# A decoder trunk on one core: the norm chains rewritten (products with the weights ahead of the factor, sums of squares by halves, GpSimd only for the power), and weight splits let three steps ahead instead of four

## The chip, the cores and the metric

The kernel runs on one core of a Trainium2 chip. Its time is the device time of one execution in microseconds (us), from the program's start to its end on that core. The engines are TensorE (PE; its weight loads are shown apart as PEld), VectorE (DVE), ScalarE (ACT), GpSimd (POOL) and SyncE (SP), which here issues transfers from HBM.

## The reference, cut to what matters

Two layers; in each an FFN, a mixer and a second FFN. Before each of the six stages the input passes through an RMS norm with weights, behind each the output passes through a second one and is added to x. x is 256 tokens by 1024, in f32.

```python
def rms_norm(x, gain):
    y = x * lax.rsqrt(jnp.mean(x * x, axis=-1, keepdims=True) + NORM_EPS)
    return y * gain
def swiglu(x, wg, wu, wd):
    return (jax.nn.silu(x @ wg) * (x @ wu)) @ wd
for l in range(DEPTH):
    x = x + 0.5 * rms_norm(swiglu(rms_norm(x, g_ffn1_pre[l]), ffn1_wg[l], ffn1_wu[l], ffn1_wd[l]), g_ffn1_post[l])
    x = x + rms_norm(hybrid_mixer(rms_norm(x, g_mix_pre[l]), ...), g_mix_post[l])
    x = x + 0.5 * rms_norm(swiglu(rms_norm(x, g_ffn2_pre[l]), ffn2_wg[l], ...), g_ffn2_post[l])
```

The mixer merges three attentions (differential, stick-breaking, block-sparse) with sigmoid gates; the change touches in it only the norm of the differential one.

## The kernel before, in words

The 256 tokens are two tiles (t = 0, 1) of 128 partitions, and x stays in SBUF as `x_73` (tile 0) and `x_74` (tile 1). The six stages are numbered n = 0 to 5; a name such as `f20Tl` says FFN (f) or mixer (m, with the layer's number), stage 2, tile 0, and the quantity. FFNs are n = 0, 2, 3, 5; the mixers are m0 (n = 1) and m1 (n = 4).

**Weights.** SP loads them in blocks of 128 x 2048 f32 (1 MB, `raw`, five buffers). Each block is split into a high and a low part, by halves of 128 x 1024: ACT copies the high part `whi` (L143), DVE subtracts for the low part `wlo` (L144). A product in f32 accuracy is three matmuls: high by high (L339), high by low (L341), low by high (L344). Activations are split in the same way after their transposition on PE: `f20p` is the transposed tile in PSUM, `f20Th` its high part (ACT, L273), `f20Tl` its low part (DVE, L274), and `f20q` a copy kept for sums (ACT, L276). The FFNs' up products of pairs of chunks are done with seven products in place of eight, for which DVE adds whole weight blocks (L134, `raw<-raw,raw`) and forms four sums of activations.

**Which split comes when.** `Stream` holds the list of uses of the weights; before each use `ahead` (L150 on) emits splits up to `AHEAD` uses ahead of the current one (L41, L154), as far as the five split buffers allow. The first five steps are in hand-written order on ACT and DVE; all else is placed by a scheduler that works by priority, which is the order of the program, except that what stands in a `soon()` block counts as if it stood 200 instructions earlier. A change of the program's order or of a chain's length so also changes which matmuls the scheduler sets between others.

**The norm chains.** `sumsq` lets ACT square a tile and accumulate the sum (two instructions, ACTIVATE and ACTIVATION_READ_ACCUMULATOR, both L229). `rstd_of` forms the factor on POOL: one `tensor_scalar` for each sum (L221: times 1/n, plus eps or plus the sum so far), then a power of -0.5 (L223). `postnorm` sums the output `acc` (PSUM) by halves, waits for the factor, forms y = acc * factor * weights (L323, a scalar_tensor_tensor of 128 x 512 for each half), then x = x + y (L325). `normed` (before an FFN) sums x in one instruction of 128 x 1024, and forms `xg` = x * factor * weights (L296, two halves); PE transposes `xg` (L271). Before a mixer, `gained` forms x * weights without the factor (L288), which is applied later (`m00r`, and `m00rq` on POOL, L711).

**Order at a stage's end.** Tile 0 of a stage ends ahead of tile 1, and tile 1's last matmuls run while tile 0's post and pre norms do; the next stage begins with tile 0's transposes, its first up products (`f20gu`), the first of the seven products (`f2c1X`), then tile 1's transposes (`f21p`). Behind an up product ACT takes the Silu `f20h` (L425) and DVE multiplies (L426).

Of the kernel before, what the change touches and what calls it, by code (L numbers as in the profile page):

```python
# [9 lines left out]
F32 = mybir.dt.float32  # L10
F32R = mybir.dt.float32r
BF16 = mybir.dt.bfloat16
AF = mybir.ActivationFunctionType
ALU = mybir.AluOpType
# [3 lines left out]
P = 128  # L18
D = 1024
# [10 lines left out]
EPS = 1e-6  # L30
# [7 lines left out]
HALF = BLK // 2  # L38
W_BUFS = 5
RAW_BUFS = 5  # L40
AHEAD = 4  # L41
LAG = 3
WARM = 18
SECOND_HALF = 2
# [8 lines left out]
HALVES = (slice(0, D // 2), slice(D // 2, D))  # L53
# [5 lines left out]
class Stream:  # L59
# [90 lines left out]
    def ahead(self, most):  # L150

        while self.done < len(self.ops) and most > 0:
            k = self.ops[self.done][0]
            if self.first[k] > self.now + AHEAD or not self.room(k):  # L154
                return
# [10 lines left out]
def trunk(ctx: ExitStack, tc, x, wall, gpre, gpost, lamv, dgain, cst, out):  # L166
    nc = tc.nc
# [3 lines left out]
    sp = ctx.enter_context(tc.tile_pool(name="act", bufs=2))  # L171
# [3 lines left out]
    def tr_tile(shape, name, tag=None):  # L175
        return ps.tile(shape, F32, tag=tag or next(tr_tags), name=name, bufs=1)
# [5 lines left out]
    xs = [cp.tile([P, D], F32, tag=f"x{t}", name=f"x{t}") for t in range(NT)]  # L182
# [14 lines left out]
    def gain(kind, i):  # L197

        if (kind, i) not in gains:
            src = gpre if kind == "pre" else gpost  # L200
            g = sp.tile([P, D], F32, tag="gain", name=f"g{kind}{i}", bufs=2)
            nc.sync.dma_start(g, bass.AP(tensor=src.tensor, offset=src.offset + i * D,
                                         ap=[[0, P], [1, D]]))
            gains[kind, i] = g
        return gains[kind, i]
# [7 lines left out]
    dg = cp.tile([P, L], F32, tag="dg", name="dg")  # L213
    nhalf = cp.tile([P, 4], F32, tag="nhalf", name="nhalf")
    nc.gpsimd.memset(nhalf, -0.5)
    def rstd_of(ssq, n, k, scale, name, tag="rstd"):

        r = sp.tile([P, k], F32, tag=tag, name=name, bufs=4)
        plus = EPS * scale ** -2
        for s in ssq:  # L220
            nc.gpsimd.tensor_scalar(r, s, scale ** -2 / n, plus, op0=ALU.mult, op1=ALU.add)  # L221
            plus = r
        nc.gpsimd.tensor_tensor(r, r, nhalf[:, :k], op=ALU.pow)  # L223
        return r

    def sumsq(src, n, name):
        junk = sp.tile([P, n], F32, tag="t4", name=name + "j", bufs=4)
        s = sp.tile([P, 1], F32, tag="ssq", name=name + "s", bufs=4)
        nc.scalar.activation(junk, src, AF.Square, accum_out=s)  # L229
        return s  # L230

    side, waiting = [], []
# [8 lines left out]
    def rest(n):  # L241
        for _ in range(n):
            yield
# [11 lines left out]
    def soon():  # L255
        return tc.high_priority(offset=SOON)

    def pair(nk, name, tag, bufs):
        if nk == 2:
            both = sp.tile([P, 2, nk, P], F32R, tag=tag, name=name, bufs=bufs)  # L260
            return [both[:, 0], both[:, 1]]
        if tag == "xT":
            return [sp.tile([P, nk, P], F32R, tag=tag + c, name=name + c, bufs=bufs) for c in "hl"]
        return [sp.tile([P, nk, P], F32R, tag=tag, name=name + c, bufs=bufs) for c in "hl"]

    def split_T(src, dst, a, n, name, keep=None):

        hi, lo = (d[:, a:a + n] for d in dst[:2])
        pt = tr_tile([P, 4, P], name, "tr" if name[0] == "f" and n == 2 else None)
        for k in range(n):  # L270
            nc.tensor.transpose(pt[:, k, :], src[:, (a + k) * P:(a + k + 1) * P], ident)  # L271
        with soon():
            nc.scalar.activation(hi, pt[:, :n], AF.Copy)  # L273
            nc.vector.tensor_sub(lo, pt[:, :n], hi.bitcast(F32))  # L274
            if keep is not None:
                nc.scalar.activation(keep[:, a:a + n], pt[:, :n], AF.Copy)  # L276
# [5 lines left out]
    xg, quads = {}, {}  # L282

    def gained(t, i, c):

        if t not in xg:
            xg[t] = sp.tile([P, D], F32, tag="t4", name=f"xg{i}{t}", bufs=4)
        nc.vector.tensor_mul(xg[t][:, c], xs[t][:, c], gain("pre", i)[:, c])  # L288

    def normed(t, i):  # L290

        with soon():
            r = rstd_of([sumsq(xs[t], D, f"n{i}{t}")], D, 1, 1.0, f"n{i}{t}r", "rpre")
            xg[t] = sp.tile([P, D], F32, tag="t4", name=f"xg{i}{t}", bufs=4)
            for c in HALVES:
                nc.vector.scalar_tensor_tensor(xg[t][:, c], xs[t][:, c], r, gain("pre", i)[:, c],  # L296
                                               op0=ALU.mult, op1=ALU.mult)

    def prenorm(t, i, name, keep=False):

        src = xg.pop(t)
        if keep:
            r, quads[t] = None, sp.tile([P, KD, P], F32, tag="t4", name=name + "q", bufs=4)
        else:
            r = rstd_of([sumsq(xs[t], D, name)], D, 1, 1.0, name + "r", "rpre")
        xT = pair(KD, name + "T", "xT", NT)
        yield xT, r
        for a in (0, 4):
            split_T(src, xT, a, 4, f"{name}p{a}", quads[t] if keep else None)
            yield  # L310

    def postnorm(t, acc, i, scale, name):

        y = sp.tile([P, D], F32, tag="t4", name=name + "y", bufs=4)
        with soon():
            r = rstd_of([sumsq(acc[:, c], D // 2, name + str(n)) for n, c in enumerate(HALVES)],
                        D, 1, scale, name + "r")
        g = gain("post", i)
        for c in HALVES:
            if c.start:  # L320
                yield
            with soon():
                nc.vector.scalar_tensor_tensor(y[:, c], acc[:, c], r, g[:, c],  # L323
                                               op0=ALU.mult, op1=ALU.mult)
                nc.vector.tensor_add(xs[t][:, c], xs[t][:, c], y[:, c])  # L325
                if i + 1 == 3 * L:
                    nc.scalar.dma_start(out[t * P:(t + 1) * P, c], xs[t][:, c])
                elif (i + 1) % 3 == 1:
                    gained(t, i + 1, c)
        if i + 1 < 3 * L and (i + 1) % 3 != 1:  # L330
            normed(t, i + 1)
        yield
# [218 lines left out]
    def groups(t):  # L551

        per = 8 // (t + 1)
        return [range(g * per, (g + 1) * per) for g in range(t + 1)]
# [36 lines left out]
    def diff_attention(y, t, l, qT, name):  # L591
        yield
        po = sp.tile([P, 4, P], F32, tag="tok", name=name + "o", bufs=4)
        for g, ms in enumerate(groups(t)):
            e, r = softmax(t, "a", qT, ms, f"{name}g{g}")
            yield from rest(REST_DIFF)
            n = len(ms) // 2
            lr = sp.tile([P, n], F32, tag="lr", name=f"{name}lr{g}")
            nc.vector.tensor_scalar(lr, r[:, 1, :], lam[:, l:l + 1], None, op0=ALU.mult)
            for i in range(n):  # L600
                nc.vector.tensor_scalar(e[:, 1, i, :], e[:, 1, i, :], lr[:, i:i + 1], None,
                                        op0=ALU.mult)
                nc.vector.scalar_tensor_tensor(e[:, 0, i, :], e[:, 0, i, :], r[:, 0, i:i + 1],
                                               e[:, 1, i, :], op0=ALU.mult, op1=ALU.subtract)
            yield
            wT = maps_T(e, range(0, 2 * n, 2), t, f"{name}T{g}")
            yield from rest(REST_MAPS)
            pa = tr_tile([P, n, P], f"{name}a{g}")
            for i in range(n):
                h = ms[0] // 2 + i  # L610
                for kb in range(t + 1):
                    nc.tensor.matmul(pa[:, i, :], wT[2 * i, kb], vS["a", kb][:, h * P:(h + 1) * P],
                                     start=kb == 0, stop=kb == t, skip_group_check=True)
            nc.scalar.activation(po[:, ms[0] // 2:ms[0] // 2 + n, :], pa, AF.Copy)
            yield
        sq = sp.tile([P, 4, P], F32, tag="tok", name=name + "sq", bufs=4)
        nc.scalar.activation(sq, po, AF.Square)
        ssq = sp.tile([P, 4], F32, tag="ssq4", name=name + "ssq")
        nc.vector.tensor_reduce(ssq, sq, axis=AX.X, op=ALU.add)
        rs = rstd_of([ssq], P, 4, 1.0, name + "rs")  # L620
        nc.vector.tensor_mul(po, po, rs[:, :, None].to_broadcast([P, 4, P]))
        yield from rest(REST_NORM)
        pt = tr_tile([P, 4, P], name + "at")
        for h in range(4):
            nc.tensor.transpose(pt[:, h, :], po[:, h, :], ident)
        nc.scalar.activation(y[0], pt, AF.Copy, scale=dg[:, l:l + 1])
        nc.vector.scalar_tensor_tensor(y[1], pt, dg[:, l:l + 1], y[0].bitcast(F32), op0=ALU.mult,
                                       op1=ALU.subtract)
# [351 lines left out]
```

## Time and profile before

| | us |
|---|---|
| three runs | 1275.62, 1277.13, 1277.08 |
| median | 1277.08 |
| profiled execution | 1277.28 |
| its span (first to last instruction) | 1275.3 |

The granted TensorE clock is 0.995 of full speed over the whole execution. In the profile's groups the largest are DVE's `wlo` (496 instructions, 588.9 us), ACT's `whi` (496, 503.2 us) and DVE's block sums (96, 115.6 us). How to read it: a group's row names line, engine, operation and operands, then busy time and the idle time of that engine just ahead of it; a row of the timeline has start and duration in us, and in brackets how long its engine had been idle and what the instruction waited for. Rows of one kind that follow on each other are drawn together (x2), with one duration over all.

### The profile page before, as it was taken

How to read it: one execution, taken by the hardware profiler on the slowest of the kernel's cores; microseconds unless marked ns; L12 is line 12 of the kernel's file. 1: busy time of each engine (PE TensorE's matmuls, PEld its weight loads, DVE VectorE, ACT ScalarE, POOL GpSimd, SP SyncE). 2: the span in 40 equal slices, each digit the busy share in tenths (PEclk: the TensorE clock that was granted, in tenths of full speed). 3: DMA queues.
4: the chain of work that ended last, by engine and by line, in shares of the span. 5: the costliest groups of instructions: out<-in, count | busy, mean ns of one | idle time of the engine just before them, and what ended most of it. 6: DMA issues, size and time to landing. Idle time of an engine off the chain costs nothing.

```text
span 1275.3 us, 15584 instructions
## 1 busy us (share of the span) xinstructions
PE 1249.8 (98%) x6034; PEld 1014.9 (80%) x6034; DVE 984.5 (77%) x1233; ACT 789.1 (62%) x1149; POOL 52.2 (4%) x82
## 2 busy tenths in 40 slices
PE   7999999999999999999999999999999999999997
PEld 4888887888877878888878888878888787788885
DVE  5999967656566589999599998666665656999982
ACT  6566655678676476666466655556885655666551
POOL 0000003000000010000010000210000000100000
PEclk8999999999999999999999999999999999999999
DMA  9465465443444434476435458454344544264550
GB/s 345 169 250 202 174 250 210 153 160 138 171 159 166 159 138 174 158 262 251 179 132 205 191 198 321 160 180 165 132 155 153 183 154 166 98 226 174 195 198 33
DMA packets 34057, 232.37 MB, mean 182 GB/s; under 512 B 3904, under 2 KB 4032, under 8 KB 6976
## 3 DMA queue, kind: packets, MB, share of 16 engines
q1 hardware_dynamic: 33264, 230.28, 49.8%
q10 hardware_dynamic: 720, 1.11, 0.2%
q8 instruction: 47, 0.77, 0.2%
q14 instruction: 26, 0.21, 0.0%
HBM read 230.33 MB, written 1.05 MB: 181 GB/s over the span
## 4 chain that ended last, share of the span: by engine, by line
PE 90%; DVE 4%; POOL 3%; issue 1%; ACT 1%; DMA 1%; SPq 0%; POOLq 0%; DVEq 0%; ACTq 0%
DVE wlo L144 1%; PE f01gu L344 1%; PE f00acc L339 1%; PE f51gu L339 1%; PE f51gu L344 1%; PE f30acc L339 1%; PE f31gu L339 1%; PE f50acc L339 1%; PE f31gu L344 1%; PE f51acc L339 1%; PE f00acc L341 1%; PE f30acc L341 1%; PE f20acc L341 1%; PE f20acc L344 1%; PE f00acc L344 1%
## 5 line engine op out<-in xcount | busy, mean ns | idle before, releaser
L144 DVE TENSOR_TENSOR wlo<-raw,whi 128x1024 fp32r<-128x1024 f32 x496 | 588.9, 1219 | 101.7 <-ACT whi L143 101.1
L143 ACT ACTIVATE whi<-raw 128x1024 fp32r<-128x1024 f32 x496 | 503.2, 1055 | 170.8 <-DVE raw L134 23.0
L134 DVE TENSOR_TENSOR raw<-raw,raw 128x1024 f32<-128x1024 f32 x96 | 115.6, 1217 | 0.0
L339 PE MATMUL f00gu<-whi,f00Th 128*128 128x512 f32 x40 | 17.2, 430 | 2.1 <-ACT f00Th L273 1.9
L721 ACT ACT_TABLE_LOAD x12 | 15.4, 1283 | 6.2 <-PE m11bg L344 2.2
L344 PE MATMUL f50gu<-whi,f50Tl 128*128 128x512 f32 x40 | 15.8, 394 | 1.2 <-DVE f50Tl L274 1.2
L344 PE MATMUL f20gu<-whi,f20Tl 128*128 128x512 f32 x40 | 15.8, 394 | 1.2 <-DVE f20Tl L274 1.2
L341 PE MATMUL f00gu<-wlo,f00Th 128*128 128x512 f32 x40 | 16.5, 412 | 0.4 <-DVE wlo L144 0.4
L344 PE MATMUL f00gu<-whi,f00Tl 128*128 128x512 f32 x40 | 16.5, 414 | 0.2 <-DVE f00Tl L274 0.2
L344 PE MATMUL f01gu<-whi,f01Tl 128*128 128x512 f32 x40 | 15.8, 394 | 0.7 <-DVE f01Tl L274 0.7
L339 PE MATMUL f00acc<-whi,f00hT 128*128 128x512 f32 x40 | 16.2, 404 | 0.0
L575 ACT ACT_TABLE_LOAD x6 | 7.7, 1283 | 13.6 <-DVE m01cg1m L570 3.6
L339 PE MATMUL f20gu<-whi,f20Th 128*128 128x512 f32 x40 | 16.1, 403 | 0.0
L339 PE MATMUL f30gu<-whi,f30Th 128*128 128x512 f32 x40 | 16.1, 403 | 0.0
L339 PE MATMUL f50gu<-whi,f50Th 128*128 128x512 f32 x40 | 16.1, 402 | 0.0
L339 PE MATMUL f30acc<-whi,f30hT 128*128 128x512 f32 x40 | 16.1, 402 | 0.0
L339 PE MATMUL f21gu<-whi,f21Th 128*128 128x512 f32 x40 | 16.0, 401 | 0.0
L339 PE MATMUL f51gu<-whi,f51Th 128*128 128x512 f32 x40 | 16.0, 400 | 0.0
L339 PE MATMUL f20acc<-whi,f20hT 128*128 128x512 f32 x40 | 16.0, 400 | 0.0
L339 PE MATMUL f31gu<-whi,f31Th 128*128 128x512 f32 x40 | 16.0, 400 | 0.0
L339 PE MATMUL f01gu<-whi,f01Th 128*128 128x512 f32 x40 | 16.0, 400 | 0.0
L339 PE MATMUL f50acc<-whi,f50hT 128*128 128x512 f32 x40 | 16.0, 399 | 0.0
(1990 smaller groups left out, 3556.6 us busy)
## 6 DMA issues: line engine op xcount, KB each, us to landing
raw<-wall_dram SPq DMA_DIRECT2D x211, 1024.0 KB, 4.8
gpre<-gpre_dram SPq DMA_DIRECT2D x6, 512.0 KB, 5.2
gpost<-gpost_dram SPq DMA_DIRECT2D x6, 512.0 KB, 4.0
raw<-wall_dram SPq DMA_DIRECT2D x2, 512.0 KB, 7.8
out_dram<-x ACTq DMA_DIRECT2D x4, 256.0 KB, 2.1
x<-x_dram SPq DMA_DIRECT2D x2, 256.0 KB, 2.9
x<-x_dram SPq DMA_DIRECT2D x1, 512.0 KB, 9.0
cs<-cst_dram SPq DMA_DIRECT2D x1, 352.0 KB, 6.3
```

The costliest lines, as they stand in the source:

```text
L134: nc.vector.tensor_add(self.raws[op[1]][:, c], self.raws[op[1]][:, c], self.raws[op[2]][:, c])
L143: nc.scalar.activation(hi, w, AF.Copy)
L144: nc.vector.tensor_sub(lo, w, hi.bitcast(F32))
L339: nc.tensor.matmul(o[:, n:n + 512], xh[:, k, :], wh[:, kk, n:n + 512], start=first, stop=False, **kw)
L341: nc.tensor.matmul(o[:, n:n + 512], xh[:, k, :], wl[:, kk, n:n + 512], start=False, stop=False, **kw)
L344: nc.tensor.matmul(o[:, n:n + 512], xl[:, k, :], wh[:, kk, n:n + 512], start=False, stop=last, **kw)
L575: nc.scalar.activation(e[:, b, i, :], s[:, b, i, :], AF.Exp, bias=mn[:, b, i:i + 1], scale=-1.0, accum_out=sm[:, b, i:i + 1])
L721: nc.scalar.activation(s, o, AF.Sigmoid, scale=r)
```

## The change

- `AHEAD` is 3 instead of 4.
- `rstd_of`: DVE's `tensor_scalar` (L219 of the changed kernel) adds eps and, where there are two sums, both sums in one instruction; POOL takes only the power. The mean's 1/n goes into the scale of ACT's Square.
- `normed`: the squares are taken by halves (two instructions of 128 x 512), and their unused output goes into `xg`'s own tile, ahead of `xg` itself.
- `postnorm`: y = acc * weights is formed ahead of the factor (L322, reads PSUM), and then one instruction makes x = y * factor + x (L327), instead of L323 and L325.

```diff
-AHEAD = 4
+AHEAD = 3
-    def rstd_of(ssq, n, k, scale, name, tag="rstd"):
+    def rstd_of(ssq, k, name, tag="rstd", eps=EPS):
         r = sp.tile([P, k], F32, tag=tag, name=name, bufs=4)
-        plus = EPS * scale ** -2
-        for s in ssq:
-            nc.gpsimd.tensor_scalar(r, s, scale ** -2 / n, plus, op0=ALU.mult, op1=ALU.add)
-            plus = r
+        nc.vector.tensor_scalar(r, ssq[0], eps, *ssq[1:] or [None], op0=ALU.add,
+                                **({"op1": ALU.add} if ssq[1:] else {}))
         nc.gpsimd.tensor_tensor(r, r, nhalf[:, :k], op=ALU.pow)
...
     def normed(t, i):
         with soon():
-            r = rstd_of([sumsq(xs[t], D, f"n{i}{t}")], D, 1, 1.0, f"n{i}{t}r", "rpre")
             xg[t] = sp.tile([P, D], F32, tag="t4", name=f"xg{i}{t}", bufs=4)
+            r = rstd_of([sumsq(xs[t][:, c], xg[t][:, c], f"n{i}{t}{n}", D ** -0.5) for n, c in enumerate(HALVES)],
+                        1, f"n{i}{t}r", "rpre")
...
     def postnorm(t, acc, i, scale, name):
+        g = gain("post", i)
         with soon():
-            r = rstd_of([sumsq(acc[:, c], D // 2, name + str(n)) for n, c in enumerate(HALVES)],
-                        D, 1, scale, name + "r")
+            f = D ** -0.5 / scale
+            r = rstd_of([sumsq(acc[:, c], junk[:, c], f"{name}{n}", f) for n, c in enumerate(HALVES)],
+                        1, name + "r", eps=EPS / scale ** 2)
+            for c in HALVES:
+                nc.vector.tensor_mul(y[:, c], acc[:, c], g[:, c])
         for c in HALVES:
             if c.start:
                 yield
             with soon():
-                nc.vector.scalar_tensor_tensor(y[:, c], acc[:, c], r, g[:, c],
-                                               op0=ALU.mult, op1=ALU.mult)
-                nc.vector.tensor_add(xs[t][:, c], xs[t][:, c], y[:, c])
+                nc.vector.scalar_tensor_tensor(xs[t][:, c], y[:, c], r, xs[t][:, c],
+                                               op0=ALU.mult, op1=ALU.add)
```

DVE gets 28 small instructions more, POOL has 40 fewer, ACT 8 more; PE has the same matmuls.

**DVE at the start of the FFN n = 2.** The stretch from tile 1's post norm of the mixer (`m01oy`) to tile 1's `xg`; `x_74` is x of tile 1, `raw` and `wlo` are weights. Before:

```order
L323 SCALAR_TENSOR_TENSOR m01oy<-m01acc,m01or,gpost_3632 128x512 x2
L325 TENSOR_TENSOR x_74<-x_74,m01oy 128x512
L274 TENSOR_TENSOR f20Tl<-f20p_3757,f20Th 128x512
L325 TENSOR_TENSOR x_74<-x_74,m01oy 128x512
L144 TENSOR_TENSOR wlo_3806<-raw_3578,whi_3805 128x1024 x2
L296 SCALAR_TENSOR_TENSOR xg_3773<-x_74,n21r,gpre_3693 128x512 x2
L134 TENSOR_TENSOR raw_3496<-raw_3496,raw_3642 128x1024
L426 TENSOR_TENSOR f20h_3801<-f20h_3801,f20gu_3776 128x256
```

The same stretch in the changed kernel:

```order
L219 TENSOR_SCALAR m01or<-m01o0s,m01o1s 128x1
L322 TENSOR_TENSOR m01oy<-m01acc,gpost_3621 128x512
L272 TENSOR_TENSOR f20Tl<-f20p_3747,f20Th 128x512
L327 SCALAR_TENSOR_TENSOR x_74<-m01oy,m01or,x_74 128x512
L322 TENSOR_TENSOR m01oy<-m01acc,gpost_3621 128x512
L144 TENSOR_TENSOR wlo_3828<-raw_3576,whi_3827 128x1024
L327 SCALAR_TENSOR_TENSOR x_74<-m01oy,m01or,x_74 128x512
L144 TENSOR_TENSOR wlo_3828<-raw_3576,whi_3827 128x1024
L134 TENSOR_TENSOR raw_3494<-raw_3494,raw_3659 128x1024
L219 TENSOR_SCALAR n21r<-n210s,n211s 128x1
L429 TENSOR_TENSOR f20h_3797<-f20h_3797,f20gu_3772 128x256
L295 SCALAR_TENSOR_TENSOR xg_3756<-x_74,n21r,gpre_3682 128x512 x2
```

`f20Tl` stands behind one small instruction and one product of a half, where it stood behind three instructions of a half; a block sum (`raw`) and the multiplication `f20h` now stand ahead of `xg`.

**PE ahead of the second half of `f20Tl`, same stage.** `f2c1X` is the first of the seven products. Before:

```order
L339 MATMUL f20gu_3776<-whi_3664,f20Th 128x512
L341 MATMUL f20gu_3776<-wlo_3665,f20Th 128x512
L339 MATMUL f2c1X<-whi_3697,f20Th 128x512
L341 MATMUL f2c1X<-wlo_3698,f20Th 128x512
L344 MATMUL f2c1X<-whi_3697,f20Tl 128x512
L339 MATMUL f2c1X<-whi_3697,f20Th 128x512
L341 MATMUL f2c1X<-wlo_3698,f20Th 128x512
L344 MATMUL f20gu_3776<-whi_3664,f20Tl 128x512
```

In the changed kernel:

```order
L342 MATMUL f20gu_3772<-whi_3686,f20Th 128x512
L344 MATMUL f20gu_3772<-wlo_3687,f20Th 128x512
L347 MATMUL f20gu_3772<-whi_3686,f20Tl 128x512
L342 MATMUL f20gu_3772<-whi_3686,f20Th 128x512
L344 MATMUL f20gu_3772<-wlo_3687,f20Th 128x512
```

The five matmuls of `f2c1X` that stood ahead of the one that needs the low part now stand behind it. Tile 1's transposes `f21p` stand four matmuls later than before in PE's order (and so they do at n = 5; at n = 3 and in the mixers their place is the same).

**PE some 20 us later in the same stage**, where the low halves of the weights come close ahead of their use. `f21acc` is the down product of tile 1. Before:

```order
L344 MATMUL f20gu_3987<-whi_3930,f20Tl 128x512
L339 MATMUL f20gu_3987<-whi_3938,f20Th 128x512
L339 MATMUL f21acc<-whi_3805,f21hT_3929 128x512
L341 MATMUL f21acc<-wlo_3806,f21hT_3929 128x512
L339 MATMUL f21acc<-whi_3805,f21hT_3929 128x512
L341 MATMUL f21acc<-wlo_3806,f21hT_3929 128x512
L339 MATMUL f2c1Y<-whi_3961,f2S2h 128x512
L341 MATMUL f20gu_3987<-wlo_3939,f20Th 128x512
```

In the changed kernel:

```order
L347 MATMUL f20gu_3983<-whi_3926,f20Tl 128x512
L342 MATMUL f20gu_3983<-whi_3934,f20Th 128x512
L344 MATMUL f20gu_3983<-wlo_3935,f20Th 128x512
L347 MATMUL f20gu_3983<-whi_3934,f20Tl 128x512
L342 MATMUL f20gu_3983<-whi_3934,f20Th 128x512
```

Five matmuls that stood ahead of the first use of the block's low part (`wlo_3939`, now `wlo_3935`) stand behind it.

## Rows read from the trace of the kernel before

**Rows 1.** The page: busy time, share and instructions of each engine.
```profile
PE 1249.8 (98%) x6034; PEld 1014.9 (80%) x6034; DVE 984.5 (77%) x1233; ACT 789.1 (62%) x1149; POOL 52.2 (4%) x82
```
**Rows 2.** Windows: us, then PE, PEld, DVE, ACT, POOL busy (count), clock, DMA, GB/s.
```profile
480.00:500.00 20.00, 20.00 (x93) 16.29 (x92) 19.60 (x26) 11.98 (x19) 0.00 (x0) 1.00 0.30 108
```
**Rows 3.** Waits of PE: what waited, for whom: us in total, times, longest.
```profile
PE f31p L271 <- DVE xg L296: 1.3, 1, 1.3
...
PE f20gu L344 <- DVE f20Tl L274: 1.2, 1, 1.2
...
PE m01p L271 <- DVE xg L288: 1.1, 1, 1.1
PE f20p L271 <- DVE xg L296: 0.9, 1, 0.9
...
PE f01gu L344 <- DVE f01Tl L274: 0.7, 1, 0.7
PE f30p L271 <- DVE xg L296: 0.7, 1, 0.7
...
PE f21p L271 <- DVE xg L296: 0.3, 1, 0.3
```
**Rows 4.** Timeline of ACT, POOL and DVE at the end of n = 0, tile 0.
```profile
186.66 0.20 ACT L229 ACTIVATION_READ_ACCUMULATOR f00o1j<-f00acc 128x1 f32 x1
...
187.39 0.54 POOL L223 TENSOR_TENSOR f00or<-f00or,nhalf 128x1 f32<-128x1 f32 x1
...
187.96 1.41 DVE L323 SCALAR_TENSOR_TENSOR f00oy<-f00acc,f00or,gpost 128x512 f32<-128x512 f32 x2 [7.02 <-POOL f00or L223]
189.29 1.28 DVE L325 TENSOR_TENSOR x<-x,f00oy 128x512 f32<-128x512 f32 x2
```
**Rows 5.** A small DVE instruction with an operand pointer; durations in ns.
```profile
L599 DVE TENSOR_SCALAR m01alr<-m01ag0r,lam x1: 229/229/229, 252.2 to 252.2; 128x2 f32<-128x2 f32 x1
```
**Rows 6.** Groups by form: a DVE instruction that reads PSUM and SBUF (us, ns).
```profile
L274 DVE TENSOR_TENSOR f20Tl<-f20p,f20Th 128x512 fp32r<-128x512 f32 x2 | 1.4, 684 | 0.0
```
**Rows 7.** Timeline of POOL and DVE behind the end of n = 0, tile 0.
```profile
191.69 4.62 DVE L144 TENSOR_TENSOR wlo<-raw,whi 128x1024 fp32r<-128x1024 f32 x4
191.93 4.44 POOL L221 TENSOR_SCALAR m00r<-m00s 128x1 f32<-128x1 f32 x1 [4.00 <-ACT m00j L229]
196.24 0.68 DVE L274 TENSOR_TENSOR m00Tl<-m00p,m00Th 128x512 fp32r<-128x512 f32 x1
196.45 0.55 POOL L223 TENSOR_TENSOR m00r<-m00r,nhalf 128x1 f32<-128x1 f32 x1
```
**Rows 8.** Timeline of ACT: the first sum for tile 1 of n = 0.
```profile
197.05 0.60 ACT L229 ACTIVATE f01o0j<-f01acc 128x512 f32<-128x512 f32 x1 [0.80 <-POOL m00r L223]
```
**Rows 9.** Timeline of DVE, start of n = 3, tile 0.
```profile
633.64 1.28 DVE L325 TENSOR_TENSOR x<-x,f20oy 128x512 f32<-128x512 f32 x2
634.84 2.35 DVE L144 TENSOR_TENSOR wlo<-raw,whi 128x1024 fp32r<-128x1024 f32 x2
637.91 1.41 DVE L296 SCALAR_TENSOR_TENSOR xg<-x,n30r,gpre 128x512 f32<-128x512 f32 x2 [0.72 <-POOL n30r L223]
```
**Rows 10.** Timeline of DVE, ACT and PE, start of n = 2, tile 1.
```profile
467.48 1.28 ACT L425 ACT_TABLE_LOAD   x1
468.77 0.39 ACT L425 ACTIVATE f20h<-f20gu 128x256 f32<-128x256 f32 x1
469.18 1.41 DVE L296 SCALAR_TENSOR_TENSOR xg<-x,n21r,gpre 128x512 f32<-128x512 f32 x2 [0.71 <-POOL n21r L223]
470.07 0.63 PE L271 MATMUL f21p<-ident,xg 128*128 128x128 f32 x4 [0.28 <-DVE xg L296]
```
**Rows 11.** Timeline of DVE and PE, n = 2: a low half and its first use.
```profile
489.86 1.21 DVE L144 TENSOR_TENSOR wlo<-raw,whi 128x1024 fp32r<-128x1024 f32 x1
491.53 0.39 PE L341 MATMUL f20gu<-wlo,f20Th 128*128 128x512 f32 x1
```
**Rows 12.** Timeline of DVE at the end of the program.
```profile
1269.50 1.41 DVE L323 SCALAR_TENSOR_TENSOR f51oy<-f51acc,f51or,gpost 128x512 f32<-128x512 f32 x2 [8.27 <-POOL f51or L223]
```

More of the change, by code (lines that the diff above doesn't have):

```diff
@@ L215, in trunk, with sumsq @@
     nc.gpsimd.memset(nhalf, -0.5)
-    def rstd_of(ssq, n, k, scale, name, tag="rstd"):
+    def rstd_of(ssq, k, name, tag="rstd", eps=EPS):
         r = sp.tile([P, k], F32, tag=tag, name=name, bufs=4)
-        plus = EPS * scale ** -2
-        for s in ssq:
-            nc.gpsimd.tensor_scalar(r, s, scale ** -2 / n, plus, op0=ALU.mult, op1=ALU.add)
-            plus = r
+        nc.vector.tensor_scalar(r, ssq[0], eps, *ssq[1:] or [None], op0=ALU.add,
+                                **({"op1": ALU.add} if ssq[1:] else {}))
         nc.gpsimd.tensor_tensor(r, r, nhalf[:, :k], op=ALU.pow)
         return r
-    def sumsq(src, n, name):
-        junk = sp.tile([P, n], F32, tag="t4", name=name + "j", bufs=4)
+    def sumsq(src, junk, name, scale):
         s = sp.tile([P, 1], F32, tag="ssq", name=name + "s", bufs=4)
-        nc.scalar.activation(junk, src, AF.Square, accum_out=s)
+        nc.scalar.activation(junk, src, AF.Square, scale=scale, accum_out=s)
         return s
@@ L304, in prenorm @@
         else:
-            r = rstd_of([sumsq(xs[t], D, name)], D, 1, 1.0, name + "r", "rpre")
+            junk = sp.tile([P, D], F32, tag="t4", name=name + "j", bufs=4)
+            r = rstd_of([sumsq(xs[t], junk, name, D ** -0.5)], 1, name + "r", "rpre")
         xT = pair(KD, name + "T", "xT", NT)
@@ L314, in postnorm @@
         y = sp.tile([P, D], F32, tag="t4", name=name + "y", bufs=4)
+        junk = sp.tile([P, D], F32, tag="t4", name=name + "j", bufs=4)
+        g = gain("post", i)
         with soon():
-            r = rstd_of([sumsq(acc[:, c], D // 2, name + str(n)) for n, c in enumerate(HALVES)],
-                        D, 1, scale, name + "r")
-        g = gain("post", i)
+            f = D ** -0.5 / scale
[3 more added lines that the diff above has]
+                nc.vector.tensor_mul(y[:, c], acc[:, c], g[:, c])
         for c in HALVES:
@@ L616, in diff_attention @@
         sq = sp.tile([P, 4, P], F32, tag="tok", name=name + "sq", bufs=4)
-        nc.scalar.activation(sq, po, AF.Square)
+        nc.scalar.activation(sq, po, AF.Square, scale=P ** -0.5)
         ssq = sp.tile([P, 4], F32, tag="ssq4", name=name + "ssq")
         nc.vector.tensor_reduce(ssq, sq, axis=AX.X, op=ALU.add)
-        rs = rstd_of([ssq], P, 4, 1.0, name + "rs")
+        rs = rstd_of([ssq], 4, name + "rs")
         nc.vector.tensor_mul(po, po, rs[:, :, None].to_broadcast([P, 4, P]))
```

## Prediction

> **What bounds the kernel now.** I read the page's busy shares first. PE is busy for 1249.8 us of a span of 1275.3, that is 98% [rows 1]. With the same matmuls before and after, only PE's 25.5 us of idle time can change the total: its waits, and the stretch behind its last matmul. The windows show where there is none to win: within an FFN PE runs without a gap, 20.00 of 20 us with 93 matmuls, so .215 us each [rows 2]. In the same window DVE is busy for 19.60 of 20, so DVE stands close behind PE there. Third, the list of PE's waits [rows 3]. Nearly all lie where one stage meets the next, and PE waits there for `xg`, the normed input, or for `f20Tl`, the low part of its transposed form. Those are the ends of the chains that the change rewrites. Three patterns repeat: `m11p` waits as `m01p` does, and the three waits of n = 5 are those of n = 2; of each one row stands.
>
> **The post chain, part by part.** From ACT's second sum to x, at the end of n = 0: the sum is there at 186.86 (186.66 + .20), DVE starts at 187.96 because it waits for POOL, and x is whole at 190.57, that is 3.71 us [rows 4]. In the changed kernel DVE adds the sums (the nearest row for such a small instruction is .23 [rows 5]), then forms two products that read PSUM and the weights; a like instruction takes .68 and a pair some 1.28, since they overlap by a little [rows 6]. POOL's power (.54 [rows 4]) runs beside them. Then two instructions x = y * factor + x follow. No row shows that form; bounds are the two rows beside it, 1.28 for the plain sum and 1.41 for the form with a factor [rows 4], and I take 1.41, since it has the same operation. Sum: .23 + 1.28 + 1.41 = 2.92 instead of 3.71, and .04 for a handover: .75 earlier. Had the power to wait for the products, it would be .23 + 1.28 + .54 + .1 + 1.41 = 3.56, a gain of .15.
>
> So does a DVE instruction hold up POOL? The rows show both. POOL's small `m00r` took 4.44 us while four `wlo` ran back to back on DVE, and ended with them; its power took .55 though `m00Tl`, which reads PSUM, ran beside it [rows 7]. The Trainium skill (page "SBUF — State Buffer", section "SBUF: two separate sides") says that a DVE operation with two SBUF inputs and a GpSimd operation that reads SBUF exclude each other for a whole instruction. By that rule the new products, with one input in PSUM, leave the power free, and the .75 stands; a reader who takes the 4.44 for a price that any long DVE instruction asks would get the .15. The trace agrees with the rule here. The third form, x = y * factor + x, has two SBUF inputs, but it runs when the power is done.
>
> **The norm chain.** At n = 3, x is whole at 634.92, `xg` starts at 637.91: 3.0 us, with a pair of splits (2.35) and .72 of idle time between [rows 9]. In the changed kernel's order one half of a split stands there instead of a pair, then the small sum (.23), then `xg`, which waits for the power (.54 and two handovers): 1.2 + .23 + .7 = 2.1, so some .9 to 1.0 earlier. At n = 2 and n = 5 the pair still stands ahead of the small sum for tile 0, and the sum, which was POOL's work beside the pair, now comes behind it: gain there none, loss up to .15. The squares by halves cost one accumulate more (.20 [rows 4]), of which about .1 is seen, since the first half runs ahead of x's second half.
>
> **What of it PE gets.**
> - Start: `f01gu` waits .7 for `f01Tl` [rows 3]. In the changed order a pair of splits that stood ahead of `f01Tl` stands behind it, so the wait goes; I take .1 off for the longer squares: .6.
> - `m01p` and `m11p`: 1.1 each [rows 3]. Tile 1's sums waited .80 for POOL's `m00r` [rows 8], which does so no more since DVE reads the sum, and the post chain gives .75: together 1.5, more than the wait. 2.2.
> - n = 2: `f20p` waits .9, `f20gu` 1.2, `f21p` .3 [rows 3]. Post less the .15 gives .6 of the first. `f20Tl` now stands behind one small instruction and one product (.9) and no longer behind three (2.1) and the wait for the factor; it comes some 2.8 earlier, and PE arrives at it earlier by the five matmuls that went behind it (5 x .215 = 1.1) and by .6. So that wait goes. But then `xg` of tile 1 is late: in the new order a block sum and `f20h` stand ahead of it, and ACT takes the second half of the squares behind the table load and the Silu (1.28 and .39 [rows 10]). I replay DVE's queue from x's first half, which comes at 463.5 if `f20Tl` comes 2.8 earlier: product .6, half a split 1.1, x .7, half a split 1.1, block sum 1.1, small sum .2, `f20h` .4; that is 468.7, and with the power some 469.05 instead of 469.18 [rows 10]. `f21p` stands four matmuls later in PE's order, so PE comes out ahead by .13 + 4 x .215 = 1.0 and not by 2.4. The rest turns into a new wait ahead of `f21p` of about 1.0.
> - n = 5: the same orders and waits, 1.0.
> - n = 3: `f30p` .7 and `f31p` 1.3 [rows 3]. Post and norm give 1.7 for each tile, with no new instruction between: both in full, 2.0.
> - The end: the last post chain starts on DVE at 1269.50 behind POOL [rows 12], nothing runs beside it, and the output follows: .75.
>
> Sum .6 + 2.2 + 1.0 + 1.0 + 2.0 + .75 = 7.55 off the profiled execution's 1277.28, which is .2 above the median of the runs: 1269.7.
>
> **Edits at no cost.** The 28 small DVE instructions (28 x .23 = 6.4 us in all) lie mostly in stretches where DVE waits for sums; without that cover they would cost at most this. ACT's eight halves lie beside splits of other blocks. `AHEAD` = 3 shifts splits by a few places on DVE and ACT, and the loads with them (SP loads when a block is freed); cover for that is the slack between a low half and its first use. The smallest that I rely on is .46: `wlo` at 489.86 ends at 491.07, PE takes it at 491.53 [rows 11].
>
> **The rivals.**
> - *DVE becomes the bound behind each start.* If PE is 1 to 2 us earlier at n = 2, 3 and 5 and DVE's low halves are not, PE loses there what is above the slack: .46 remains of each, so .6 + 2.2 + 3 x .46 + .75 = 4.9, 1272.4. For it speaks DVE's 19.60 of 20 [rows 2] and that five matmuls ahead of `wlo_3939`'s use went behind. Against it, at n = 2 and 5 one block sum (1.2) is done ahead of `xg`, and the next one comes later, so DVE has less to do up to that place.
> - *The power doesn't run beside the products.* Then post gives .15. `m01p` and `m11p` still have the .80 and get .95 each; n = 2 and 5 keep .4 each (1.0 less the .6 that post loses), n = 3 some 1.8 by the norm part, the end .15: .6 + 1.9 + .8 + 1.8 + .15 = 5.25, 1272.0. The rows on `m00Tl` speak against it [rows 7].
> - *The splits come one use later, and slower comes out.* `AHEAD` = 3 lets a split be placed one use later, a use being 12 matmuls, 12 x .215 = 2.6 us. Where DVE has no free time PE would then wait 2.6 - .46 = 2.1 once in each of n = 2, 3 and 5, 6.4 in all, and what was won at those starts would be void, since PE would wait for the splits anyway: 6.4 - (.6 + 2.2 + .75) = 2.8 slower, 1280.1. It decides once the low halves in that stretch move back by more than .46. Against it: the orders show `wlo` at nearly the same places between the same neighbours as before.
>
> **How the numbers follow.** Forecast .64, the first rival .18, the power .08, the later splits .10. A change of .2% (2.5 us) is what a measurement of this kernel can tell from none. Faster needs less than 1274.5: the forecast nearly whole (.61 of .64), the first rival .13, the power .06, together .80. Same: .03 + .05 + .02 from these and .02 from the later splits, .12. Slower: .08. The range begins at 1265.5, where all waits in the list of rows 3 and their repeats would be gone (some 10.5) and the end gains .9, and a little more; it ends at 1275.5, which takes in the two middle rivals with their own spread. The forecast alone: 1267.5 to 1272.
>
> **What would show it.** Right: POOL's work falls to the power, of about .55 each time, and DVE's first product runs beside it; no wait of PE at `m01p`, `m11p`, `f30p`, `f31p`; no wait at `f20gu` for `f20Tl`, but one of about 1 us at `f21p` and `f51p`; x whole some 2.9 us behind the last sum at the end. Wrong: waits of PE for `wlo` behind the starts of n = 2, 3, 5 (first or third rival, by size: under 1 or over 2 us each), or powers of 1.3 us and more (second). The forecast as a whole fails if PE's idle time falls by less than 4 us.

## The result and the profile after

The changed kernel takes 1267.36 us in the median of four runs (1266.59 to 1268.09), the kernel before 1276.43 beside it; the ratio is 0.9929 with a 95% interval of 0.9912 to 0.9946. The forecast was 1269.7. The profiled executions are 1268.09 (span 1266.1) and 1277.28: 9.2 us, where 7.55 had been forecast. Two executions of the experiments are far longer than the others of their kernels and are left out below: one of 1391.99 us in e_no_halves_products_first, and one of 6463.84 in e_halves_not_at_3, whose only profile it is.

The page's busy times of the changed kernel, then its waits of PE from the first up products on (which engine and line waited for what, us in total, times, longest):

```profile
PE 1249.3 (99%) x6034; PEld 1014.8 (80%) x6034; DVE 986.7 (78%) x1261; ACT 788.6 (62%) x1165; POOL 26.9 (2%) x42
```
```profile
PE f00gu L342 <- ACT whi L143: 1.0, 1, 1.0
PE f2c1X L342 <- ACT f2c1s L468: 0.7, 1, 0.7
PE f5c1X L342 <- ACT f5c1s L468: 0.7, 1, 0.7
PE f30gu L344 <- DVE wlo L144: 0.6, 1, 0.6
PE f30hp L269 <- ACT f31q L274: 0.4, 1, 0.4
...
PE f20p L269 <- DVE xg L295: 0.2, 1, 0.2
```

PE's work is the same as in [rows 1]; POOL's has halved. ACT has 16 instructions more (1165 for 1149 on the pages), two for each of the eight added halves. Of the waits in [rows 3] only `f20p`'s is left, with .2. In their place stand waits of two new kinds: for ACT's copy `f2c1s`, and at n = 3 for `f31q` and a low part of the weights.

Where the time came from is read best as a shift: how much earlier the same group of matmuls ends (at n = 2, 3, 5 the last one of tile 0's down product), in the timelines of before and after, stage by stage. The start counts from the first transposes, since the loads ahead of them land up to 1.9 us apart from one execution to another, whatever the kernel. Away from the starts of the stages the shift stands still: it is 2.64 at `m01p` and 2.65 at the mixer's last matmul some 236 us later, so the granted clock (0.995 and 0.997 over the whole) has no part in it. The last row is the changed kernel run once more (e_after_again).

```
us           n=0   m01p   n=2    n=3   m11p   n=5    end    sum
forecast     .6    1.1    1.0    2.0   1.1    1.0    .75    7.55
measured    1.34   1.30   1.86   .79   1.36   1.64  1.07    9.4
again       1.35   1.30   1.82   .84   1.37   1.64  1.07    9.4
```

The end of n = 0, tile 0, in the changed kernel (timeline of ACT, DVE and POOL; [rows 4] are the same place before):

```profile
185.41 0.20 ACT L227 ACTIVATION_READ_ACCUMULATOR f00oj<-f00acc 128x1 f32 x1
...
185.64 0.21 DVE L219 TENSOR_SCALAR f00or<-f00o0s,f00o1s 128x1 f32<-128x1 f32 x1 [5.95 <-ACT f00oj L227]
185.77 1.28 DVE L322 TENSOR_TENSOR f00oy<-f00acc,gpost 128x512 f32<-128x512 f32 x2
...
185.93 0.54 POOL L221 TENSOR_TENSOR f00or<-f00or,nhalf 128x1 f32<-128x1 f32 x1 [167.54 <-DVE f00or L219]
...
186.96 1.41 DVE L327 SCALAR_TENSOR_TENSOR x<-f00oy,f00or,x 128x512 f32<-128x512 f32 x2
```

From the sum (185.61) to x (188.37) it is 2.76 us instead of 3.71. POOL's power lies whole beside the two products; DVE has no idle time between them and x.

### The profile page after: what moved, and what is told of

Read it like the earlier page. It is cut to its first block, busy times and chain, and to the rows that moved or that the text cites. A ratio compares the mean times of both kernels' runs of the same rounds, so it can differ in the third digit from the quotient of the medians.

```text
span 1266.1 us, 15569 instructions
## 1 busy us (share of the span) xinstructions
PE 1249.3 (99%) x6034; PEld 1014.8 (80%) x6034; DVE 986.7 (78%) x1261; ACT 788.6 (62%) x1165; POOL 26.9 (2%) x42
## 4 chain that ended last, share of the span: by engine, by line
PE 96%; DMA 2%; DVE 1%; ACT 1%; issue 0%; SPq 0%; POOL 0%; DVEq 0%
DMA raw<-wall_dram 2%; PE f20gu L347 1%; PE f50gu L347 1%; PE f01gu L342 1%; PE f20gu L342 1%; PE f00acc L342 1%; PE f50acc L342 1%; PE f20acc L342 1%; PE f50gu L342 1%; PE f21gu L347 1%; PE f01gu L347 1%; PE f51gu L347 1%; PE f51gu L342 1%; PE f21gu L342 1%; PE f00acc L344 1%; PE f21acc L342 1%
## 5 line engine op out<-in xcount | busy, mean ns | idle before, releaser
L344 PE MATMUL f30gu<-wlo,f30Th 128*128 128x512 f32 x40 | 15.7, 393 | 0.6 <-DVE wlo L144 0.6
L342 PE MATMUL f31acc<-whi,f31hT 128*128 128x512 f32 x40 | 16.0, 399 | 0.0
L342 PE MATMUL f21acc<-whi,f21hT 128*128 128x512 f32 x40 | 15.9, 397 | 0.0
```

What stands on the lines that cost most here:

```text
L342: nc.tensor.matmul(o[:, n:n + 512], xh[:, k, :], wh[:, kk, n:n + 512], start=first, stop=False, **kw)
L344: nc.tensor.matmul(o[:, n:n + 512], xh[:, k, :], wl[:, kk, n:n + 512], start=False, stop=False, **kw)
```

## The experiments

All carry the times of runs beside runs of the kernel before on the same chip. The shifts below come from their profiles, reckoned as above.

**The parts one by one.** `AHEAD` alone:

```diff
-AHEAD = 4
+AHEAD = 3
```


> The kernel before with AHEAD = 3 and nothing else. Theory 1 (the gain is the shorter norm chains, which PE waits for where stages meet): only the order of splits moves; at the start the wait of .7 for f01Tl goes, the waits at m01p, m11p, f30p, f31p stay (4.3 together): 0.5 to 1.5 us faster than before. Theory 2 (the gain is a matter of order: splits let later make room for f20Tl and xg): 4 us or more faster, the waits at n = 2 and n = 5 gone.

Measured: 1274.35, ratio .9988 (.9979 to .9997). The shift is 1.18 at the start and .3 over all the rest: the wait for `f01Tl` is gone, and those at the other starts stand as before:

```profile
PE f31p L271 <- DVE xg L296: 1.3, 1, 1.3
PE f50gu L344 <- DVE f50Tl L274: 1.2, 1, 1.2
PE f20gu L344 <- DVE f20Tl L274: 1.2, 1, 1.2
```

So `AHEAD` is the start's gain and hardly any other, as theory 1 had it; theory 2 falls.

Sums on DVE alone:

```diff
-            nc.gpsimd.tensor_scalar(r, s, scale ** -2 / n, plus, op0=ALU.mult, op1=ALU.add)
+        nc.vector.tensor_scalar(r, ssq[0], eps, *ssq[1:] or [None], op0=ALU.add, ...)
```


> Only the sums go to DVE and POOL takes only the power; AHEAD = 4, products and squares as before. Theory 1: the sums of tile 1 no longer wait for POOL's m00r and m10r (.8 each), and the small sum is some .2 shorter than POOL's way in each post chain; where it stands behind a pair of splits the norm chain loses up to .15: 1.5 to 3 us faster. Theory 2: within 1 us of before.

Measured: 1276.54, ratio 1.0002 (.9993 to 1.0011), shift 1.08 in all (.37 at `m01p`, .40 at `m11p`, .85 at n = 3, losses of .5 in each mixer). The median shows none of it; in the profiled executions 2.5 us lie outside the span, and 2.0 before. This was a miss for theory 1: `m01p` still waits .8, and ACT still stands idle .78 ahead of tile 1's first sum (.80 in [rows 8]). So POOL didn't hold up these sums.

Sums and product, `AHEAD` = 4, squares in one piece (the diff of the change without its first line and without the part in `normed`):

> Sums on DVE and the post norm's product ahead of the factor; AHEAD = 4, squares in one piece. Theory 1: each post chain is shorter by .75 to .8 in all, so m01p and m11p wait no more (2.3), the end is 1.0 shorter, n = 2, 3 and 5 win .6 to .8 for each tile: 5 to 7 us faster. Theory 2: under 3 us faster.

Measured: 1266.88, ratio .9933 (.9919 to .9947), shift 8.25, more than the 5 to 7 expected. The product is the part that matters. Then the whole change but `AHEAD`:

> The whole change with AHEAD = 4 (sums, products, squares by halves). Theory 1: all of the gain but that of the start (1.2 of 9.1): 7 to 8 us faster than before, and without the wait of .6 for a low half at n = 3 if that comes from the later splits. Theory 2: at most half of the gain, 4.5 us.

Measured: 1269.26, ratio .9949 (.9937 to .9962), shift 7.14: the squares by halves make it no better. Against e_sums_and_post they give 1.0 more at n = 2, and take .4 at n = 5 and 1.35 at n = 3, where the waits for `f31q` and a low part show up with either `AHEAD`. So those waits don't come from `AHEAD` = 3.

The product alone, with sums and power on POOL:

```diff
         with soon():
             r = rstd_of([sumsq(acc[:, c], D // 2, name + str(n)) for n, c in enumerate(HALVES)], D, 1, scale, name + "r")
+            for c in HALVES:
+                nc.vector.tensor_mul(y[:, c], acc[:, c], g[:, c])
...
-                nc.vector.scalar_tensor_tensor(y[:, c], acc[:, c], r, g[:, c], op0=ALU.mult, op1=ALU.mult)
-                nc.vector.tensor_add(xs[t][:, c], xs[t][:, c], y[:, c])
+                nc.vector.scalar_tensor_tensor(xs[t][:, c], y[:, c], r, xs[t][:, c], op0=ALU.mult, op1=ALU.add)
```


> The kernel before (AHEAD = 4, sums and power on POOL, squares in one piece) with only the post norm's product formed ahead of the factor. Theory 1 (the product leaves the chain whoever forms the sum, since it reads PSUM and doesn't hold POOL): at the end x comes 2.5 behind the last sum instead of 3.7, and the total is 5 to 8 us below before; m01p and m11p may keep a small wait, since tile 1's sums still wait for POOL's m00r. Rival (the product only pays together with the sums on DVE): under 3 us faster.

Measured: 1266.17, ratio .9925 (.9912 to .9939), shift 9.79. It is more than expected: this one edit gains as much as the whole change, though it has none of the start's gain. Its end (ACT, DVE, POOL):

```profile
1258.09 0.20 ACT L229 ACTIVATION_READ_ACCUMULATOR f51o1j<-f51acc 128x1 f32 x1
...
1258.32 1.29 DVE L320 TENSOR_TENSOR f51oy<-f51acc,gpost 128x512 f32<-128x512 f32 x2 [8.27 <-ACT f51o1j L229]
...
1258.46 0.27 POOL L221 TENSOR_SCALAR f51or<-f51o1s,f51or 128x1 f32<-128x1 f32 x1 [0.47 <-ACT f51o1j L229]
1258.81 0.54 POOL L223 TENSOR_TENSOR f51or<-f51or,nhalf 128x1 f32<-128x1 f32 x1
...
1259.53 1.40 DVE L325 SCALAR_TENSOR_TENSOR x<-f51oy,f51or,x 128x512 f32<-128x512 f32 x2
```

All of POOL's work behind the last sum (till 1259.35) fits beside the products (till 1259.6), and x is whole 2.64 behind the last sum, where it was 3.71. So moving the sums off POOL has nothing left to win; with them on DVE as well (e_sums_and_post) the shift is 1.5 smaller.

**Does the power run beside the product?** The changed kernel with the product formed from the squares in SBUF:

```diff
-                nc.vector.tensor_mul(y[:, c], acc[:, c], g[:, c])
+                nc.vector.tensor_mul(y[:, c], junk[:, c], g[:, c])
```


> The changed kernel with the post norm's product formed from the squares in SBUF instead of the stage's output in PSUM (the output is left out of the product); order and sizes as before. Theory 1 (a DVE instruction with two SBUF inputs holds POOL, one with a PSUM input doesn't): at m01, f21, m11, where both products stand behind the sum, POOL's power takes 1.2 us or more instead of .55 and x starts .6 or more later behind the sum. Theory 2 (the power runs beside any DVE instruction, and the 4.4 us of m00r had another cause): .55 as before.

In the changed kernel, at n = 2, tile 1 (POOL):

```profile
458.85 0.54 POOL L221 TENSOR_TENSOR m01or<-m01or,nhalf 128x1 f32<-128x1 f32 x1 [6.79 <-DVE m01or L219]
```

With the product from SBUF (DVE and POOL):

```profile
459.06 1.28 DVE L322 TENSOR_TENSOR m01oy<-m01oj,gpost 128x512 f32<-128x512 f32 x2
460.77 1.41 DVE L327 SCALAR_TENSOR_TENSOR x<-m01oy,m01or,x 128x512 f32<-128x512 f32 x2 [0.43 <-POOL m01or L221]
...
459.21 1.52 POOL L221 TENSOR_TENSOR m01or<-m01or,nhalf 128x1 f32<-128x1 f32 x1 [7.92 <-DVE m01or L219]
```

The product takes 1.28 either way. With one input in PSUM the power is done in .54; with both in SBUF it ends only behind the products, after 1.52, and DVE then waits .43 for it. At `f21` it is 1.45, at `m11` 1.52. The Trainium skill (page "SBUF — State Buffer", section "SBUF: two separate sides") has this exclusion, and the trace agrees.

At `f21`, where DVE's order is the same, x starts 1.71 behind the first product instead of 1.20, so .5 later, a little less than expected. The kernel takes 1270.61 (one run), and the shift falls to 6.93, 2.4 less; the prediction's rival of a power that doesn't run beside the products had put that at 2.3. n = 2 and n = 5 keep .53 and .28, but not by POOL alone: there the scheduler also sets `f20Tl` and `f50Tl` behind x again, and PE waits 1.2 for each, as before the change.

**The product still earlier.** Without the halves, and with both products ahead of DVE's sum:

```diff
-            r = rstd_of([sumsq(...) ...], 1, name + "r", eps=EPS / scale ** 2)
+            ss = [sumsq(acc[:, c], junk[:, c], f"{name}{n}", f) for n, c in enumerate(HALVES)]
             for c in HALVES:
                 nc.vector.tensor_mul(y[:, c], acc[:, c], g[:, c])
+            r = rstd_of(ss, 1, name + "r", eps=EPS / scale ** 2)
```


> As e_no_halves (AHEAD = 3, squares in one piece), and in the post norm both products stand ahead of DVE's small sum, so that they run while ACT still sums. Theory 1: at the end, where nothing else runs, the products (1.28) leave the chain and the power (.55, two handovers) takes their place: the stretch behind PE's last matmul falls from 7.2 to 6.6 or 6.7; the starts of n = 3 and 5 change by under .5: .3 to 1.2 us faster than e_no_halves. Rival: where DVE is full the products only change place with the splits, and what the scheduler moves costs more than .5: no faster, or slower.

Measured: 1271.11, ratio .9963 (.9949 to .9976), 5.9 slower than the same kernel with the sum first (e_no_halves below). Its end:

```profile
1261.60 0.20 ACT L227 ACTIVATION_READ_ACCUMULATOR f51oj<-f51acc 128x1 f32 x1
...
1261.84 1.29 DVE L321 TENSOR_TENSOR f51oy<-f51acc,gpost 128x512 f32<-128x512 f32 x2 [7.34 <-ACT f51oj L227]
1263.04 0.20 DVE L219 TENSOR_SCALAR f51or<-f51o0s,f51o1s 128x1 f32<-128x1 f32 x1
1263.97 1.41 DVE L327 SCALAR_TENSOR_TENSOR x<-f51oy,f51or,x 128x512 f32<-128x512 f32 x2 [0.72 <-POOL f51or L221]
```

The expectation fell, and shows why the order matters: the product doesn't run beside ACT's sums at all. It waits on a semaphore until ACT has read `f51acc` (1261.80), so the small sum and the power come one after another behind it: x is there 3.6 after the sum (1265.38), nearly as before the change. The Trainium skill (page "PSUM — Partial Sum Buffer", section "PSUM bank collisions raise a hardware error") gives a reason for such a wait: two engines must not access one PSUM bank of the same partitions at once, reads included. The trace agrees so far as the wait is there; it is for the whole tile, since the product of the first half stands still as well until ACT has read the second (1261.80; the first by 1261.22). So here too the power lies outside the products, and the shift is 5.4 instead of 11.3.

**Why n = 3 gave less.** Three runs. Squares in one piece everywhere, `AHEAD` = 3:

> The whole change with AHEAD = 3, but the squares of the norm ahead of an FFN in one piece. Theory 1 (behind the start of n = 3 DVE becomes the bound: squares by halves bring xg there earlier than DVE can deliver the low parts): no wait for f31q, f3S1l or a low half at n = 3; from the first transposes to the end within 1 us of the changed kernel, either side, since n = 2 and n = 5 lose what the halves gave there. Theory 2 (halves and AHEAD = 3 each give their own part): 1 to 2 us slower than the changed kernel.

```diff
-            r = rstd_of([sumsq(xs[t][:, c], xg[t][:, c], ...) for n, c in enumerate(HALVES)], 1, f"n{i}{t}r", "rpre")
+            r = rstd_of([sumsq(xs[t], junk, f"n{i}{t}", D ** -0.5)], 1, f"n{i}{t}r", "rpre")
```

Measured: 1265.19, ratio .9917 (.9903 to .9931), shift 11.3 of which n = 3 has 2.39; the waits for `f31q` and the low part are gone, as theory 1 had it. But the total is 1.9 better than the changed kernel's, where theory 1 had put it within 1 us: without the halves n = 2 loses nothing (1.93) and n = 5 wins (2.0). Only at n = 3 in one piece (`if i == 3:` around the same edit):

> The whole change, but at n = 3 the squares are in one piece. Theory 1: n = 2 and n = 5 as in the changed kernel, n = 3 without its three waits behind the start (1.8 us of shift) but with one of about .5 for xg at f31p: 1 to 1.5 us faster than the changed kernel, 10 to 10.5 faster than before. Theory 2: .5 slower than the changed kernel.

Measured: 1265.03 (five runs within 1.8 us), ratio .9919 (.9905 to .9932), 10.8 faster than before. Its waits are not known. And the changed kernel with less work for DVE there:

```diff
+            if (op[1], op[2]) != (LAYER_BLKS + 2, LAYER_BLKS + 5):
                 nc.vector.tensor_add(self.raws[op[1]][:, c], self.raws[op[1]][:, c], self.raws[op[2]][:, c])
```


> The changed kernel without one block sum on DVE (two instructions of 128 x 1024, 2.4 us) in the first seven products of n = 3; that part of the computation is left out. Theory 1 (DVE's work is the bound there): the three waits of PE behind the start of n = 3 (for f31q, f3S1l and a low half) are gone, and PE is 1.5 to 1.8 us earlier at the end of n = 3. Theory 2 (the waits come from where the scheduler set the matmuls): they stay, within .3 of the changed kernel.

Measured: 1265.62 (one run); no wait of PE at n = 3, shift there 2.45 instead of .79. At n = 3 that is the size of theory 1, but the run doesn't show its cause. With one sum left out, the scheduler drew the next block sum forward into its place: from `xg` of tile 1 to `f31q` DVE has the same twelve instructions in both kernels (11.0 us of work), with .30 of idle time between them instead of 1.80. What differs is a load, as the chain of waits of the changed kernel shows (start us, us, what):

```profile
646.87 7.02 DMA raw<-wall_dram
653.92 1.07 ACT whi L143
655.01 1.22 DVE wlo L144
656.23 0.60 DVE f31q L411
656.84 1.14 DVE wlo L144
658.00 5.04 DMA raw<-wall_dram
663.07 1.06 ACT whi L143
...
665.64 1.15 DVE wlo L144
666.83 0.50 PE f30gu L344
```

A load stands in it twice. SP's issues in the changed kernel, then in e_no_halves:

```profile
645.70 0.33 SPq L202 DMA_DIRECT2D gpre<-gpre_dram  x1
646.87 33.31 SPq L112 DMA_DIRECT2D raw<-wall_dram  x5
```
```profile
643.05 0.33 SPq L112 DMA_DIRECT2D raw<-wall_dram  x1
645.18 0.33 SPq L202 DMA_DIRECT2D gpre<-gpre_dram  x1
```

With the halves, the scheduler sets the second half of one split behind `xg` of tile 1 (both halves stood ahead of it), so that the block is freed later. Its successor's load is issued 2.6 behind `xg`'s start (644.26) instead of .7 ahead of it (643.74 in e_no_halves), 3.3 us later in the chain, and behind the load of the norm's weights; it takes 7.02 us to land, and 4.8 in e_no_halves. In e_less_dve_at_3 it is issued just as late (645.96, also 2.6 behind `xg`'s start at 643.35), but lands in 5.52. DVE waits for it that much less (DVE of the changed kernel; then the load and DVE of e_less_dve_at_3):

```profile
655.01 1.22 DVE L144 TENSOR_TENSOR wlo<-raw,whi 128x1024 fp32r<-128x1024 f32 x1 [1.80 <-ACT whi L143]
```
```profile
645.96 5.52 DMA raw<-wall_dram
```
```profile
652.60 1.23 DVE L144 TENSOR_TENSOR wlo<-raw,whi 128x1024 fp32r<-128x1024 f32 x1 [0.30 <-ACT whi L143]
```

So PE's wait for `f31q` follows the load: it is .43 where the load lands 9.6 us behind `xg`'s start (the changed kernel), .17 where it lands 9.4 behind (e_after_again, 6.80 to land), and none at 8.1 (e_less_dve_at_3) and 4.1 (e_no_halves). Behind the load DVE runs with hardly any idle time up to the low part that PE waits for. Whether a DVE with less work would make up for a late load was not tried, nor why the load took 5.5 us in one kernel and 7 in the other.

**The least that does it, and the change once more.** The kernel before with the product ahead and `AHEAD` = 3, nothing else:

> The kernel before with two edits only: the post norm's product formed ahead of the factor, and AHEAD = 3; sums and power stay on POOL, squares in one piece. Theory 1 (the product and, at the start, AHEAD carry the gain; the sums on DVE and the halves bring nothing): the two waits at the start (.4 and .7) go as in e_ahead3_only, the rest stays as in e_products_pool_sums: 1264.3 to 1265.8, as fast as e_no_halves and 1 to 2.5 us faster than the changed kernel. Rival (AHEAD = 3 only fits together with the sums on DVE): 1266 or more.

Measured: 1265.13, ratio .9909 (.9893 to .9926), shift 11.8. It is as fast as e_no_halves with two edits instead of three.

> The changed kernel once more, beside the other two on the same chip: 9 us faster than before, the two levels of 1266.6 and 1268.1 of its runs explained by when the first loads land; 1.5 to 2.5 slower than the kernel with squares in one piece.

Measured: 1266.81, ratio .9929 (.9916 to .9941), 9.1 faster than before and 1.6 slower than e_no_halves, as expected. Its profiled execution is 1.3 shorter than the first of this kernel, and its first transposes begin 1.3 earlier (7.98, 9.28), which bears out the part on the loads. The intervals of this kernel and the one with two edits overlap; that the two edits are better than the whole change rests on the profiles, 11.8 against 9.4 and 9.4 us of shift, and on n = 3 in them, 1.92 against .79 and .84.

## Why the prediction was right, point by point

- **The post chain: right, a little small.** 3.71 became 2.76, .95 and not .75: the form x = y * factor + x took the 1.41 that was chosen, but the small sum and the first product overlap (.13 from start to start instead of .23), and so do the products and x. The end has the same .95, and 1.07 with the output behind it, instead of .75.
- **The power beside the product: right,** and shown by its reverse (.54 against 1.52). Powers of 1.46 to 2.59 us, which the prediction gave as a sign of the rival, are left in the mixers' own norms (`m00r`, `m01r`, `m10r`, `m11r`), beside `wlo`; none is in a post chain.
- **`m01p` and `m11p`: right in size** (1.30 and 1.36, the whole wait), wrong in one reason. The .80 in [rows 8] was no hold by POOL: ahead of that sum both POOL's `m00r` (197.00) and PE's last matmul of the tile (196.93) end within .12 us, and in the changed kernel the same idle time of ACT is there, put down to PE:

```profile
195.78 0.60 ACT L227 ACTIVATE f01oj<-f01acc 128x512 f32<-128x512 f32 x1 [0.73 <-PE f01acc L380]
```

  With POOL still doing the sums (e_products_pool_sums), `m01p` and `m11p` win 1.30 and 1.36 too. The product alone is enough.
- **The start:** .6 forecast, 1.34 measured; the wait of .4 of `f00gu` for its low part, of which I had said nothing, went with the .7 of `f01Tl`. e_ahead3_only has 1.18 of it.
- **n = 2 and n = 5:** forecast 1.0, measured 1.86 and 1.64. That `f20Tl`'s wait goes was right. The step that failed is the replay of DVE up to `xg` of tile 1, which gave it .13. It starts at 466.07, 3.1 earlier than in [rows 10], of which 2.6 had been won before the stage, so .5; its steps from x's first half on took 5.45 for 5.55 forecast, and the rest is that x was there .3 sooner. And the new wait is not at `f21p`: `f2c1X` waits .7 for ACT to copy the product before it out of PSUM, and behind that `f21p` finds `xg` ready.

```profile
465.34 0.60 ACT L468 ACTIVATE f2c1s<-f2c1X 128x512 f32<-128x512 f32 x1 [1.39 <-PE f2c1X L347]
465.99 0.50 PE L342 MATMUL f2c1X<-whi,f20Th 128*128 128x512 f32 x1 [0.69 <-ACT f2c1s L468]
466.07 1.41 DVE L295 SCALAR_TENSOR_TENSOR xg<-x,n21r,gpre 128x512 f32<-128x512 f32 x2 [0.33 <-POOL n21r L221]
```

- **n = 3: the term that was wrong.** "Both in full, 2.0" held up to tile 1's transposes, where PE is 2.6 ahead of the stage's beginning; 1.8 was given back within 20 us, and .79 was left. The first rival had named the place and the sign, a wait for `wlo` under 1 us, and its .46 for what would remain is not far from .79, but its reason was not what the chain begins with: a load that a moved half split let go late. No run shows that DVE's own work was the bound there; and n = 2 and n = 5, where that rival expected the same, have no wait for `wlo`. The sentence on `AHEAD` counted loads as covered by the slack of a low half; the halves, not `AHEAD`, moved one past that.
- **The norm chain:** counted as a gain of .9 at n = 3. Without the halves n = 3 wins 2.4, with them .8: as a part of this change they cost 1.6 there, and 2 us of the total.
- **The later splits** (slower) did not come: `AHEAD` = 3 alone is faster.

The sum came out 1.8 too small: n = 0, 2 and 5 gave .7, .9 and .6 beyond the forecast and the other places .8, which outweighs n = 3 (-1.2). That terms wrong in both directions nearly met is luck. The median of 1267.36 is inside the range, and .1 below the narrower one that the prediction gave for its forecast alone (1267.5 to 1272). One sum in it is off: [rows 3] with their repeats add up to 9.7 and not to some 10.5, which would have set the lower end of the range at 1266.3.

## What to carry to other kernels

When an engine waits for a small factor, do ahead of it what doesn't need the factor, and choose the form by what the engine that makes the factor shares with it: here a product that reads PSUM hid the whole factor, and the same product from SBUF held it up. Try the parts of a change apart: two of the four here carried everything, one was worth nothing and one cost 2 us. And when a chain gets shorter, look at what the scheduler now sets behind its end: a split moved by one place let a load go 3.3 us later.

## What the runs showed of the hardware that was not expected

Where a load of 512 KB had been issued 1.17 us ahead of it, a load of 1 MB took 7.02 and 6.80 us from issue to landing in the two profiles of the changed kernel, and 5.52 in e_less_dve_at_3; the median of such loads before was 4.8. What sets it within that range is not known.

An idle time of PE costs more than its own length, since its matmuls overlap in the trace: in a row they start .23 us apart, though each is drawn .39 long. From the last matmul ahead of the wait of .43 for `f31q` to the second one of `f30acc` behind it the changed kernel needs 1.33 us (654.69 to 656.02), and e_less_dve_at_3, which has the same instructions without the wait, .68. So the wait cost .65. The two steps across the wait of .61 for the low part take 1.33 as well (665.83 to 667.17), where two steps otherwise take .45: .88.
